# A layer with 32 experts on one core: expert lists from a table, biases with 128 rows, weight splits of 2048 columns, steps in pairs of PSUM banks

## The chip, the core and the metric

One core of a Trainium2 chip runs the whole layer in one launch. The metric is the device time in microseconds (us). The engines are TensorE (PE: matmuls, with their weight loads shown apart as PEld), VectorE (DVE), ScalarE (ACT), GpSimd (POOL) and SyncE (SP, which issues most of the transfers). Each runs its own instructions in order.

## What is computed

A sequence of 1024 tokens of width 1024 goes through a mixer (a state-space scan beside windowed attention) and then through a mixture of experts. The change concerns the experts only:

```
logits = xf @ w_router + b_router                     # 1024 tokens, 32 experts
top_v, top_i = top_k(logits, 4);  gates = softmax(top_v)
# for each expert e, over the tokens that chose it (sorted by expert, in blocks of 128)
gu = xb @ w_gate_up[e] + b_gate_up[e]                 # 1024 x 2048
glu, lin = split(gu);  glu = min(glu, 7);  lin = clip(lin, -7, 7)
act = glu * sigmoid(1.702 * glu) * (lin + 1)
y = act @ w_down[e] + b_down[e]                       # 1024 x 1024
out[token] += y * gate
```

All in float32; the kernel keeps that precision on PE by splitting each operand into a high and a low part and taking three products of them.

## The kernel before

The mixer, the router and the ranking of the experts by their counts of tokens take the first 1100 us or so. Then `moe` goes through the 32 experts in the order `ORDER`, which takes by turns one with many tokens and one with few. CAPS gives each rank its number of rows: 15 experts have more than 128 (two row blocks, "wide"), 17 have 128 ("narrow"). The last three of the order are narrow.

Each expert is 12 steps, c = 0 to 11: eight for gate and up, four for down. A step works on one chunk of weights of 1 MB. `Weights.fetch` brings a chunk in two halves (buffers raw, eight of them, filled by SP's transfers), and `Weights.prepare` in step c makes the parts of chunk c + 3: for each half of 1024 columns ACT copies hi (L1491) and DVE subtracts to get lo (L1493). The parts have four buffers, so the hi of a step begins when PE is through with the product of the step before.

In a narrow expert the rows are the stationary operand: `up` (L1306, L1307, L1309 in `product`) multiplies the chunk into one bank of PSUM, two steps to a bank, 12 matmuls of 512 columns a step. A bias matmul ends the second of them (L1320, 64 rows: hi and lo parts of 32 biases, picked by the column `pick`). `act` then reads the bank: after a gate bank ACT takes the sigmoid (L1339) and DVE multiplies (L1341); after an up bank DVE clips and multiplies (L1344, L1345), which gives um. In steps 5 and 9 PE transposes um (`turn`, L1277), and ACT and DVE split it into `a` (L1284, L1286). `down` multiplies `a` with the down weights, and `store` scales y by the gate and g2 (L1440) and adds the rows to acc_d by a scatter of POOL (L1442). In steps 1, 6, 7 and 10 PE transposes the next expert's rows x, which POOL has gathered (L1255). In a wide expert the weights are stationary (`up_wide`, L1359 and L1360, two banks a step), and `act_wide` reads the two banks in the step after.

The list of an expert (which tokens, where to add, gates) is made two experts ahead: `places` compares positions with iota on DVE (L1197, eight operations), `slots` multiplies this with the table info on PE (L1213, 8 matmuls of 6 columns for a narrow expert, 16 for a wide one) and sums up with seven small DVE operations for each row block (L1217 to L1226).

The order of PE, DVE and ACT within the stage is the order in which the code is written (a manual schedule): in each step `before`, then a `weave` of the store, `after`, `prepare` and the split of x, then `main`. `weave` takes one piece of each job by turns. The waits between engines are set by tile: an instruction that writes a tile waits for those that still read what it holds. PSUM holds eight banks: five for the products (pool emm), two for transposes (etp), one for slots (elg).

## Time and profile before

| | |
|---|---|
| median of 3 runs | 2746.44 us (2744.35 to 2754.49) |
| the profiled execution | 2748.94 us, span 2746.8 us |
| PE busy in the span | 2513.2 us (91%), 14030 matmuls |
| DVE busy | 2190.4 us (80%) |
| ACT busy | 1471.6 us (54%) |
| POOL busy | 273.7 us (10%) |
| transfers | 662.57 MB, mean 241 GB/s |

Shares over the whole span mix stages with different limits, so they say little. The expert stage lies between about 1105 and 2680 us, and is to be read by itself, in windows of it and in the timeline of one expert. A matmul's duration in a row is longer than the distance to the next one, since they are pipelined: what a matmul costs is read from start to start.

### The profile page before, as it was taken

The page shows a single profiled execution, that of the slowest core. Times are in us where ns is not written, and L with a number is a line of the kernel's source. Part 1 is how long each engine was busy: PE and PEld are TensorE (multiplying, and loading weights), DVE is VectorE, ACT ScalarE, POOL GpSimd, SP SyncE. Part 2 cuts the span into 40 slices and gives each one's busy share as a digit, 9 for nine tenths or more (in the row PEclk, how much of TensorE's full clock was granted, in tenths as well). Part 3 has the DMA queues.
Part 4 walks back from the last instruction along what each step waited for, and adds up shares of the span by engine and source line. Part 5 has one row for each costly group of instructions (what it writes and reads, how often), then busy time and mean ns, then how long its engine had stood idle before and what let it go on. Part 6 is the DMA issues. An engine that isn't in the chain of part 4 may idle for free. (4 is left out here: it accounts for less than half of the span.)

```text
span 2746.8 us, 41465 instructions
## 1 busy us (share of the span) xinstructions
PE 2513.2 (91%) x14030; PEld 2113.3 (77%) x14030; DVE 2190.4 (80%) x4354; ACT 1471.6 (54%) x2394; POOL 273.7 (10%) x173
## 2 busy tenths in 40 slices
PE   6799999889989886899999999999999999999990
PEld 1598887767778775788878878888988887888770
DVE  9735797348787757787987987988989899989995
ACT  0622112657766312555665665666666666666661
POOL 3300000000000004010100100111011011101113
PEclk8799999999999876899999999999999999999995
DMA  7434623644686782797987987998998999899984
GB/s 250 163 121 145 209 92 114 181 160 156 229 303 242 278 294 97 238 287 218 299 266 239 306 271 243 308 300 252 301 305 269 288 310 306 274 298 303 311 279 146
DMA packets 400937, 662.57 MB, mean 241 GB/s; under 512 B 36976, under 2 KB 203760, under 8 KB 393616
## 3 DMA queue, kind: packets, MB, share of 16 engines
q1 hardware_dynamic: 388416, 615.83, 67.0%
q0 software_dynamic: 11872, 42.47, 6.7%
q8 instruction: 112, 1.84, 0.3%
q10 hardware_dynamic: 432, 1.57, 0.2%
q14 instruction: 105, 0.86, 0.1%
HBM read 570.63 MB, written 89.15 MB: 240 GB/s over the span
## 5 line engine op out<-in xcount | busy, mean ns | idle before, releaser
L1493 DVE TENSOR_TENSOR wl<-raw,wh 128x1024 fp32r<-128x1024 f32 x768 | 921.6, 1220 | 162.4 <-ACT wh L1491 161.4
L1491 ACT ACTIVATE wh<-raw 128x1024 fp32r<-128x1024 f32 x768 | 789.6, 1052 | 244.0 <-PE dn L1309 88.7
L1359 PE MATMUL uw<-x,wh 128*128 128x320 f32 (+5 forms) x1920 | 578.3, 365 | 0.2 <-issue 0.2
L1360 PE MATMUL uw<-x,wl 128*128 128x192 f32 (+4 forms) x1920 | 500.2, 261 | 0.0
L1359 PEld LDWEIGHTS uw<-x,wh 128*128 128x128 f32 x1920 | 363.1, 189 | 23.5 <-issue 0.3
L1360 PEld LDWEIGHTS uw<-x,wl 128*128 128x128 f32 x1920 | 368.2, 192 | 0.5
L1306 PE MATMUL dn<-wh,a 128*128 128x512 f32 (+4 forms) x752 | 298.7, 397 | 0.0
L1307 PE MATMUL dn<-wl,a 128*128 128x512 f32 (+4 forms) x752 | 293.5, 390 | 0.0
L1309 PE MATMUL dn<-wh,a 128*128 128x512 f32 (+3 forms) x608 | 238.5, 392 | 0.6 <-DVE a L1286 0.6
L1306 PE MATMUL up<-wh,x 128*128 128x512 f32 x544 | 221.8, 408 | 0.0
L1442 POOL DMA_INDIRECT acc_d<-y,wi x47 | 118.9, 2531 | 959.5 <-DVE y L1440 815.8
L1309 PE MATMUL up<-wh,x 128*128 128x512 f32 x544 | 213.0, 392 | 0.0
L1307 PE MATMUL up<-wl,x 128*128 128x512 f32 x544 | 212.3, 390 | 0.0
L1371 ACT ACTIVATE t<-uw,bias 128x160 f32<-128x160 f32 (+5 forms) x240 | 98.6, 419 | 131.8 <-PE uw L1360 130.9
L1306 PEld LDWEIGHTS dn<-wh,a 128*128 128x128 f32 (+4 forms) x752 | 135.7, 180 | 37.8 <-issue 4.1
L1307 PEld LDWEIGHTS dn<-wl,a 128*128 128x128 f32 (+4 forms) x752 | 135.8, 181 | 33.8
L1309 PEld LDWEIGHTS dn<-wh,a 128*128 128x128 f32 (+3 forms) x608 | 112.8, 186 | 28.4 <-DVE a L1286 2.7
L1306 PEld LDWEIGHTS up<-wh,x 128*128 128x128 f32 x544 | 102.3, 188 | 27.4 <-issue 8.4
L1309 PEld LDWEIGHTS up<-wh,x 128*128 128x128 f32 x544 | 102.1, 188 | 22.4
L1307 PEld LDWEIGHTS up<-wl,x 128*128 128x128 f32 x544 | 102.4, 188 | 18.8
L51 PE MATMUL mm<-whi,uh 128*128 128x256 f32 x320 | 108.4, 339 | 4.4 <-DVE r L307 4.4
L52 PE MATMUL mm<-wlo,uh 128*128 128x256 f32 x320 | 107.7, 337 | 0.0
(529 smaller groups left out, 4970.7 us busy)
## 6 DMA issues: line engine op xcount, KB each, us to landing
raw<-w_gate_up SPq DMA_DIRECT2D x512, 512.0 KB
raw<-w_down SPq DMA_DIRECT2D x256, 512.0 KB
mw<-w_mod SPq DMA_DIRECT2D x64, 256.0 KB
raw<-w_in SPq DMA_DIRECT2D x13, 1024.0 KB
whi<-wo SPq DMA_DIRECT2D x10, 1024.0 KB
wlo<-wo SPq DMA_DIRECT2D x10, 1024.0 KB
raw<-w_mod SPq DMA_DIRECT2D x8, 1024.0 KB
gate_d<-gs SPq DMA_DIRECT2D x16, 512.0 KB
```

The source lines that it names most:

```text
L51: nc.tensor.matmul(out, lhsT=lsel(lh, k), rhs=rsel(rh, k), start=start and k == 0, stop=False)
L52: nc.tensor.matmul(out, lhsT=lsel(lh, k), rhs=rsel(rl, k), start=False, stop=False)
L1306: nc.tensor.matmul(ps, lhsT=h, rhs=wh[:, k], start=st, stop=False)
L1307: nc.tensor.matmul(ps, lhsT=h, rhs=wl[:, k], start=False, stop=en and nb <= 64)
L1309: nc.tensor.matmul(ps, lhsT=X[:, k0 + k, lo:lo + nb], rhs=wh[:, k], start=False, stop=en)
L1359: nc.tensor.matmul(p[:, 0:2 * n], lhsT=wh[:, k, fs], rhs=self.x[:, k, 0:2 * n], start=k == 0, stop=False)
L1360: nc.tensor.matmul(p[:, 0:m], lhsT=wl[:, k, fs], rhs=self.x[:, k, 0:m], start=False, stop=k == KT - 1)
L1371: nc.scalar.activation(out=y[i], in_=self.uw[i][:, 1], func=ACTF.Identity, bias=self.bias[:, q * 8 + j0 + i:q * 8 + j0 + i + 1])
L1442: nc.gpsimd.indirect_dma_start(out=K.acc_d, out_offset=bass.IndirectOffsetOnAxis(ap=wi[0:nb], axis=0), in_=o[0:nb], in_offset=None, bounds ...
L1491: nc.scalar.activation(out=h, in_=r, func=ACTF.Copy)
L1493: nc.vector.tensor_tensor(l, r, h, ALU.subtract)
```

## The change

- **Lists.** A table list_d in DRAM with 1280 rows of four numbers for each expert is filled with a default at the start. `spread`, in pieces between the steps of the first experts, computes on DVE where each token stands in the lists of its four experts, and POOL scatters the rows (32 scatters of 128 rows of 16 bytes; each waits for the one before). From the seventh expert on, the list is read from the table by one transfer of SP for each row block, and `places` and `slots` are not called. The first six are made as before.
- **Biases.** The bias operands get 128 rows in place of 64, the upper 64 zero.
- **lo.** The two halves of hi stay, the two subtractions become one of 2048 columns after both. The raw buffers hold whole chunks: four in place of eight halves.
- **Pairs.** The products' PSUM becomes three tiles of two banks. `up` writes its first bank in steps 0, 1 (4, 5) and its second in steps 2, 3 (6, 7); a narrow `down` writes the two halves of y to the two banks of one tile; `up_wide` fills one tile a step, and `act_wide` handles both banks by one operation where it had two. The extra bank for slots is gone.

```diff
+    K.list_d = dram.tile([32 * LIST, 4], I32, name="list_d")
...
+LIST = 1280
+FIRST = 6
...
+    nc.sync.dma_start(out=K.list_d, in_=a["lists"])
...
+def spread(tc, K, pool):
...
+    v.scalar_tensor_tensor(key, K.posr, 0.0, base.unsqueeze(1).to_broadcast([128, 8, 32]), ALU.is_gt, ALU.mult)
...
+    for t in range(8):
+        yield
+        v.tensor_tensor(oh, key[:, t].unsqueeze(1).to_broadcast([128, 4, 32]), mx[:, t, 0:4].unsqueeze(2).to_broadcast([128, 4, 32]), ALU.is_equal)
+        v.tensor_tensor(oh, oh, K.gr[:, t].unsqueeze(1).to_broadcast([128, 4, 32]), ALU.mult)
+        yield
+        v.reduce_sum(pay[:, t, :, 2].bitcast(F32), oh, axis=AX.X)
+        for j in range(4):
+            nc.gpsimd.indirect_dma_start(out=K.list_d, out_offset=bass.IndirectOffsetOnAxis(ap=idx[:, t, j:j + 1], axis=0),
+                                         in_=pay[:, t, j], in_offset=None, bounds_check=32 * LIST - 1, oob_is_err=True)
+            yield
...
-            s = P.pk.tile([64, 256], F32R, tag="pk", name="pk")
-            nc.vector.tensor_scalar(s, K.full, self.pick, None, ALU.mult)
-            self.sel = s[:, 0:128] if self.n == 128 else s[:, 128:256]
+            self.sel = P.pk.tile([128, 128], F32R, tag="pk", name="pk")
+            nc.vector.tensor_scalar(self.sel, K.full, self.pick, None, ALU.mult)
...
+    def banks(self, name):
+        return self.K.mm.tile([128, 2, 512], F32, tag="mm", name=name)
...
-        if c % 2 == 0:
-            self.gu = K.mm.tile([128, 512], F32, tag="mm", name="up")
-        p = self.gu
+        if c % 4 == 0:
+            self.both = self.banks("up")
+        p = self.gu = self.both[:, c // 2 % 2]
...
-        for i in range(2):
-            v.tensor_tensor(x[i], self.uw[i][:, 0], y[i], ALU.add)
+        v.tensor_tensor(x, uw[:, :, 0:n], y, ALU.add)
...
-            self.y.append([self.K.mm.tile([128, 512], F32, tag="mm", name="dn")[0:nb if nb > 64 else 2 * nb] for nb in self.blocks])
+            if self.wide or c == 0:
+                self.dn = self.banks("dn")
+            self.y.append([self.dn[0:nb if nb > 64 else 2 * nb, b if self.wide else c] for b, nb in enumerate(self.blocks)])
...
-        for i in range(2):
-            ks = slice(i * kn, (i + 1) * kn)
-            h, l, r = (x.rearrange("p k n -> p (k n)") for x in (hi[:, ks], lo[:, ks], self.raw.pop(0)))
-            nc.scalar.activation(out=h, in_=r, func=ACTF.Copy)
-            h = h.bitcast(F32)
-            nc.vector.tensor_tensor(l, r, h, ALU.subtract)
-            yield
+        h, l, r = (x.rearrange("p k n -> p (k n)") for x in (hi, lo, raw))
+        for i in (0, 1024):
+            nc.scalar.activation(out=h[:, i:i + 1024], in_=r[:, i:i + 1024], func=ACTF.Copy)
+            if i == 0:
+                yield
+        nc.vector.tensor_tensor(l, r, h.bitcast(F32), ALU.subtract)
+        yield
...
-    P.ahead = 8 if deep else 4
+    P.ahead = 4 if deep else 2
...
-        K.mm = pool(es, "emm", 5, space=PSUM)
+        K.mm = pool(es, "emm", 3, space=PSUM)
         K.tp = pool(es, "etp", 2, space=PSUM)
-        K.lg = pool(es, "elg", 1, space=PSUM)
...
+                    nc.sync.dma_start(out=x[0:nb], in_=K.list_d[r * LIST + b * 128:r * LIST + b * 128 + nb])
...
-                        weave(prev.store(1) if c == 0 and prev else None, cur.after(c), W.prepare(), x)
+                        weave(prev.store(1) if c == 0 and prev else None, cur.after(c), W.prepare(), x, limit(to_lists, 2))
```

The order of instructions shows what the pairs do. A name has its buffer's number behind it, and what stands in brackets is the engines or queues that the instruction waits for. **PE, from step 5 to step 6 of a narrow expert, before:**

```order
L1307 MATMUL up_23162<-wl_23098,x_22386 128x512
L1309 MATMUL up_23162<-wh_23097,x_22386 128x512
L1320 MATMUL up_23162<-bgu_10327,pk_22966 128x512
L1277 MATMUL tp_23226<-ident_60,x_22894 128x128 [waits PE_49]
L1277 MATMUL tp_23226<-ident_60,x_22894 128x128 x3
L1306 MATMUL up_23246<-wh_23130,x_22386 128x512 [waits Activation_49]
```

**And in the change**, the same place (L1361 is the bias matmul, L1315 the transposes of the next x, L1344 the first matmul of `main`):

```order
L1345 MATMUL up_21361<-wl_21312,x_20726 128x512
L1347 MATMUL up_21361<-wh_21311,x_20726 128x512
L1361 MATMUL up_21361<-bgu_10330,pk_21187 128x512
L1315 MATMUL tp_21404<-ident_60,x_21121 128x128 [waits PE_49]
L1315 MATMUL tp_21404<-ident_60,x_21121 128x128 x3
L1344 MATMUL up_21361<-wh_21332,x_20726 128x512 [waits DVE_49]
```

The product of step 6 had a tile of its own (up_23246) and its first matmul waited for ACT's hi; now it goes to the other bank of the tile up_21361 that the bias has just finished, and it waits for DVE. From step 1 to step 2 it is the same without the transposes.

**PE, from step 10 to step 11 of the same expert, before:**

```order
L1306 MATMUL dn_23306<-wh_23268,a_23065 128x512
L1307 MATMUL dn_23306<-wl_23269,a_23065 128x512
L1309 MATMUL dn_23306<-wh_23268,a_23065 128x512
L1306 MATMUL dn_23336<-wh_23296,a_23065 128x512
L1307 MATMUL dn_23336<-wl_23297,a_23065 128x512
```

**And in the change:**

```order
L1344 MATMUL dn_21477<-wh_21442,a_21282 128x512
L1345 MATMUL dn_21477<-wl_21443,a_21282 128x512
L1347 MATMUL dn_21477<-wh_21442,a_21282 128x512
L1344 MATMUL dn_21477<-wh_21468,a_21282 128x512 [waits DVE_49]
L1345 MATMUL dn_21477<-wl_21469,a_21282 128x512
```

The second half of y had a tile of its own (dn_23336) and no wait at its first matmul; now both halves are in dn_21477, and the first matmul of step 11 waits for DVE.

**DVE, from step 1 to step 2 of the same expert, before:**

```order
L1493 TENSOR_TENSOR wl_22006<-raw_21891,wh_22005 128x1024 [waits DMAHW2_49,Activation_49]
L1493 TENSOR_TENSOR wl_22006<-raw_21893,wh_22005 128x1024 [waits DMAHW3_49,Activation_49]
L1286 TENSOR_TENSOR x_21994<-tp_21995,x_21994 128x4x128 [waits PE_49]
L1493 TENSOR_TENSOR wl_22033<-raw_21925,wh_22032 128x1024 [waits DMAHW4_49,PE_49,Activation_49]
L1341 TENSOR_TENSOR t_22026<-up_21981,t_22026 128x512
L1493 TENSOR_TENSOR wl_22033<-raw_21927,wh_22032 128x1024 [waits DMAHW5_49,Activation_49]
```

**And in the change** (L1531 is lo, L1324 the lo part of the next x, L1382 the multiplication by the sigmoid):

```order
L1531 TENSOR_TENSOR wl_21287<-raw_21179,wh_21286 128x2048 [waits DMAHW4_49,DMAHW5_49,PE_49,Activation_49]
L1324 TENSOR_TENSOR x_21276<-tp_21277,x_21276 128x4x128 [waits PE_49]
L1382 TENSOR_TENSOR t_21306<-up_21263,t_21306 128x512 [waits Activation_49]
L1531 TENSOR_TENSOR wl_21312<-raw_21211,wh_21311 128x2048 [waits DMAHW6_49,DMAHW7_49,PE_49,Activation_49]
L1531 TENSOR_TENSOR wl_21333<-raw_21244,wh_21332 128x2048 [waits DMAHW0_49,DMAHW1_49,PE_49,Activation_49]
```

Ahead of L1382 stood half a lo of its own step, and half of the one before; now a whole lo of the step before and the copy of x stand there, and the lo of its own step comes behind it.

## Rows read from the trace of the kernel before

**Rows 1.** Windows: one stretch of the expert stage, with the columns.
```profile
core 0: us, PE busy (x) PEld busy (x) DVE busy (x) ACT busy (x) POOL busy (x), PEclk, DMA share, GB/s
1200.00:1400.00 200.00, 199.12 (x1049) 165.51 (x1048) 166.47 (x290) 118.32 (x168) 17.93 (x11) 1.00 0.84 265
```

**Rows 2.** PE's waits, 1150 to 2680 us: in total, times, longest.
```profile
PE tp L1277 <- DVE t L1345: 4.6, 15, 0.3
```

**Rows 3.** Windows over one narrow expert, 2002.38 to 2041.83, the sum.
```profile
sum 39.45, PE 39.15 PEld 30.20 DVE 38.47 ACT 28.16 POOL 6.09; mean PE 9.79 PEld 7.55 DVE 9.62 ACT 7.04 POOL 1.52
```

**Rows 4.** Timeline of PE around a bias matmul (start, duration in us).
```profile
2008.08 0.39 PE L1309 MATMUL up<-wh,x 128*128 128x512 f32 x1
2008.39 0.49 PE L1320 MATMUL up<-bgu,pk 64*128 64x512 f32 x1
...
2009.15 0.39 PE L1307 MATMUL up<-wl,x 128*128 128x512 f32 x1
...
2011.89 0.39 PE L1307 MATMUL up<-wl,x 128*128 128x512 f32 x1
```

**Rows 5.** Windows, PE at the slots matmuls (L1213) alone, from the seventh expert's list.
```profile
1340.00:2600.00 1260.00, 23.99 (x304) 1.00 0.90 284
```

**Rows 6.** Timeline of PE: transposes of um behind a slots group, next matmul.
```profile
2018.41 0.66 PE L1277 MATMUL tp<-ident,t 128*128 128x128 f32 x4 [0.30 <-DVE t L1345]
2018.83 0.47 PE L1306 MATMUL up<-wh,x 128*128 128x512 f32 x1
```

**Rows 7.** Timeline of DVE in the same narrow expert.
```profile
2007.64 2.35 DVE L1493 TENSOR_TENSOR wl<-raw,wh 128x1024 fp32r<-128x1024 f32 x2
2009.91 0.68 DVE L1286 TENSOR_TENSOR x<-tp,x 128x512 fp32r<-128x512 f32 x1
2010.51 1.21 DVE L1493 TENSOR_TENSOR wl<-raw,wh 128x1024 fp32r<-128x1024 f32 x1
2011.64 0.68 DVE L1341 TENSOR_TENSOR t<-up,t 128x512 f32<-128x512 f32 x1
...
2041.55 0.74 DVE L1440 SCALAR_TENSOR_TENSOR y<-dn,gt,g 128x512 f32<-128x512 f32 x1
```

**Rows 8.** Timeline of ACT in the same narrow expert.
```profile
2005.36 1.06 ACT L1491 ACTIVATE wh<-raw 128x1024 fp32r<-128x1024 f32 x1 [0.48 <-ACT wh L1491]
...
2006.94 1.05 ACT L1491 ACTIVATE wh<-raw 128x1024 fp32r<-128x1024 f32 x1
2008.92 0.60 ACT L1339 ACTIVATE t<-up 128x512 f32<-128x512 f32 x1 [0.93 <-PE up L1320]
...
2019.11 0.60 ACT L1284 ACTIVATE a<-tp 128x512 fp32r<-128x512 f32 x1 [2.51 <-PE tp L1277]
2019.60 2.00 ACT L1491 ACTIVATE wh<-raw 128x1024 fp32r<-128x1024 f32 x2
```

**Rows 9.** Timeline of PE: two idle times of the mixer (in brackets).
```profile
288.70 0.35 PE L51 MATMUL mm<-whi,uh 128*128 128x256 f32 x1 [2.53 <-DVE r L307]
...
501.46 0.68 PE L458 MATMUL yp<-wo,ss 128*128 128x128 f32 x4 [1.92 <-DMA wo<-wout_d]
```

**Rows 10.** Windows with the granted clock (PEclk): behind these two, and in the expert stage.
```profile
288.70:292.10 3.40, 3.40 (x18) 3.40 (x19) 2.56 (x7) 0.00 (x0) 0.00 (x0) 0.58 0.57 147
501.50:505.00 3.50, 3.50 (x27) 3.32 (x28) 0.75 (x2) 0.76 (x1) 0.00 (x0) 1.00 0.69 214
1873.00:1876.50 3.50, 3.50 (x15) 3.50 (x14) 3.15 (x10) 1.88 (x4) 1.07 (x1) 0.51 0.86 267
```

**Rows 11.** Timeline of POOL: lists of the third expert done; the third expert's scatter.
```profile
1147.61 1.00 POOL L1255 DMA_INDIRECT x<-xm_d,ri  x1 [31.46 <-DVE L L1217]
...
1296.03 2.33 POOL L1442 DMA_INDIRECT acc_d<-y,wi  x1 [34.87 <-DVE y L1440]
```

**Rows 12.** POOL's gathers (L1255), then its adding scatters (L1442): issue to landing.
```profile
DMA to landing us min/median/max: 4.0/5.9/8.2
...
DMA to landing us min/median/max: 6.0/9.5/12.7
```

More of the change, by code (lines that the diff above doesn't have):

```diff
@@ L1101, in rank_consts @@
     K.eid = late.tile([1, 32], I32, name="eid")
-    K.pick = late.tile([64, 32], F32, name="pick")
+    K.pick = late.tile([128, 32], F32, name="pick")
+    v.memset(K.pick[64:128], 0.0)
     K.cnt = late.tile([64, 32], F32, name="cnt")
@@ L1186, in rank_gates @@
     v.tensor_copy(gr, p)
+    K.gr = pool.tile([128, 8, 32], F32, bufs=1, name="gr0")
+    nc.scalar.activation(out=K.gr, in_=p, func=ACTF.Copy)
     for j in range(3):
@@ L1335, in act @@
         nc, P, nb = self.nc, self.P, self.n
-        x = self.whole(self.gu, nb, ("hg", "hu")[q])[0:nb]
-        t = P.tmp.tile([128, 512], F32, tag=("sg", "um")[q], name="t")[0:nb]
+        x = self.gu[0:nb]
+        t = P.tmp.tile([128, 2, 512], F32, tag=("sg", "um")[q], name="t")[0:nb, 0]
         if q == 0:
@@ L1353, in up_wide @@
         wh, wl = w
-        self.uw = []
+        t = self.banks("uw")
         for i in range(2):
-            p = K.mm.tile([128, 512], F32, tag="mm", name="uw")
+            p = t[:, i]
             fs = slice(i * 128, (i + 1) * 128)
@@ L1461, in add @@
         for m, kn, k, c in WIDE if wide else CHUNKS:
-            self.todo += [(eid, m, kn // 2, k + i * kn // 2, c) for i in range(2)]
+            self.todo.append((eid, m, kn, k, c))
     def fetch(self):
@@ L1473, in fetch @@
         w = w.rearrange("e (p k) n -> p (e k) n", p=128) if m == "w_gate_up" else w.rearrange("e (k p) n -> p (e k) n", p=128)
-        nc.sync.dma_start(out=r, in_=w[:, k:k + kn])
+        for h in range(0, kn, kn // 2):
+            nc.sync.dma_start(out=r[:, h:h + kn // 2], in_=w[:, k + h:k + h + kn // 2])
         self.raw.append(r)
@@ L1586, in expert_consts @@
     nc = tc.nc
-    K.bgu = late.tile([64, 2 * D], F32R, name="bgu")
-    K.full = late.tile([64, 256], F32, name="full")
+    K.bgu = late.tile([128, 2 * D], F32R, name="bgu")
+    K.full = late.tile([128, 128], F32, name="full")
     nc.gpsimd.memset(K.full, 1.0)
-    nc.gpsimd.memset(K.full[:, 192:256], 0.0)
-    br = K.wp.tile([128, KT, 256], F32, tag="raw", name="br").rearrange("p k n -> p (k n)")[0:64]
+    br = K.wp.tile([128, KT, 256], F32, tag="raw", name="br").rearrange("p k n -> p (k n)")
+    nc.gpsimd.memset(br[64:128], 0.0)
     for j in range(2):
         nc.sync.dma_start(out=br[j * 32:(j + 1) * 32], in_=a["b_gate_up"])
-    nc.gpsimd.tensor_scalar(br[:, D:], br[:, D:], 1.0, 1.0, ALU.add, ALU.mult)
+    nc.gpsimd.tensor_scalar(br[0:64, D:], br[0:64, D:], 1.0, 1.0, ALU.add, ALU.mult)
     for c in range(4):
@@ L1618, in expert_id, with table @@
                 if r not in regs:
-                    regs[r] = nc.sync.value_load((eid if P.ahead == 8 else K.eid)[0:1, r:r + 1], min_val=0, max_val=31)
+                    regs[r] = nc.sync.value_load((eid if P.ahead == 4 else K.eid)[0:1, r:r + 1], min_val=0, max_val=31)
                 return regs[r]
             def place(i):
-                if i < len(ORDER):
+                if i < FIRST:
                     r = ORDER[i]
                     return places(tc, K, P.li, lambda t: K.posr[:, t, r:r + 1], CAPS[r])
+            def table(r):
+                out = []
+                for b, nb in enumerate(BLOCKS[CAPS[r]]):
+                    x = P.li.tile([128, 4], I32, tag="tab%d" % b, name="tab")
+                    nc.sync.dma_start(out=x[0:nb], in_=K.list_d[r * LIST + b * 128:r * LIST + b * 128 + nb])
+                    out.append((x[:, 0:1], x[:, 1:2], x[:, 2:3].bitcast(F32)))
+                yield out
             def lists(i, o, *steps):
@@ L1629, in lists @@
                     r = ORDER[i]
-                    return slots(tc, K, P.li, K.lg, o, lambda t: K.info[:, t, r, :], BLOCKS[CAPS[r]], *steps)
+                    return table(r) if i >= FIRST else slots(tc, K, P.li, K.tp, o, lambda t: K.info[:, t, r, :], BLOCKS[CAPS[r]], *steps)
             def start(i, ls):
@@ L1638, in start @@
                 return e
-            P.ahead = 2
+            P.ahead = 1
             with tc.manual_schedule(engines={mybir.EngineType.PE, mybir.EngineType.DVE, mybir.EngineType.Activation}):
@@ L1648, in moe @@
                 regs.clear()
-                P.ahead = 8
+                P.ahead = 4
                 for x in cur.x_parts():
@@ L1658, in moe @@
             prev = None
+            to_lists = spread(tc, K, P.li)
             with tc.manual_schedule(engines={mybir.EngineType.PE, mybir.EngineType.DVE, mybir.EngineType.Activation}):
@@ L1748, in rest @@
             v.tensor_copy(inf[:, :, 3:6], K.info[:, :, 0, 3:6])
-            pk = sm.tile([64, 1], F32, tag="pk", name="pk")
-            v.tensor_tensor(pk, K.route[0:64, 65:66], row[0:64, 33:34], ALU.is_equal)
+            pk = sm.tile([128, 1], F32, tag="pk", name="pk")
+            v.memset(pk[64:128], 0.0)
+            v.tensor_tensor(pk[0:64], K.route[0:64, 65:66], row[0:64, 33:34], ALU.is_equal)
             W = Weights(tc, a, P)
             W.add(eid)
-            e = Expert(tc, K, P, (128,), pk, next(slots(tc, K, P.li, K.lg, places(tc, K, P.li, lambda t: pos[:, t:t + 1], 128),
+            e = Expert(tc, K, P, (128,), pk, next(slots(tc, K, P.li, K.tp, places(tc, K, P.li, lambda t: pos[:, t:t + 1], 128),
                                                         lambda t: inf[:, t, :], (128,))))
```

64 lines of the change are left out of this document (38 added, 26 removed).

## The prediction

> **What bounds the kernel now.** I read the windows of the expert stage first. TensorE (PE) is busy 199.12 of 200 us at the full clock, VectorE (DVE) 166.47, ScalarE (ACT) 118.32 [rows 1]. The list of PE's waits over the whole stage has one entry worth naming, 4.6 us in 15 places, none over 0.3 us [rows 2]. So the stage is PE's queue laid end to end: time is won only by taking something off that queue, and whatever makes PE wait is added in full. In a narrow expert (39.45 us) DVE is busy 38.47 us as well [rows 3]. The reader should keep that in mind: a new wait of PE on DVE meets an engine with a full queue.
>
> **The change, part by part.** The sum is made against the profiled execution, 2748.94 us, which is 2.5 us above the median of the three runs.
>
> *Bias with 128 rows.* A plain matmul of 512 columns costs 0.228 us: twelve of them start between 2009.15 and 2011.89. From the last one before a 64-row bias matmul (2008.08) to the second one after it (2009.15) are 1.07 us, where three plain ones take 0.68 [rows 4]. So 0.39 us is lost around it. There are 4 in each of 17 narrow experts; with 128 rows I take it that they become plain matmuls: 68 x 0.39 = **-26.2 us**.
>
> *Lists from the table.* From the seventh expert on, the slots matmuls go: 304 in the rows, 23.99 us of PE [rows 5], **-24.0**. With them goes most of the wait in front of the transposes of um, 0.30 us where it is shown [rows 6]; of the 4.6 us I take **-4.0**. places and the small list operations leave DVE, which gives no time by itself, as PE does not wait for them. What spread adds to DVE lies in the first three experts, where DVE has 33 us free in 200 [rows 1]: nothing, and if that cover were gone, at most its own length on DVE. The fill of list_d is one early transfer. SP's 38 table reads stand among the weight fetches of step 5 and wait for the last scatter alone, which must have landed long before the fifth expert: nothing on SP, nothing for the fetches behind them. The 32 scatters of GpSimd (POOL) are a rival, below.
>
> *lo in one piece of 2048 columns.* Two pieces of 1024 take 2.27 us from start to start (2007.64 to 2009.91), one of 512 takes 0.60 (2009.91 to 2010.51) [rows 7]: 0.065 fixed plus 0.535 for each 512, so 2.21 for 2048. The 0.06 saved is DVE's, not PE's: nothing. But the piece starts only after both halves of hi. At the very first chunk nothing hides that: one half of hi, 1.06 [rows 8], **+1.1**. A raw buffer now comes free by whole chunks, one half piece (1.1 us) later; with four chunks ahead, some 13 us of a narrow expert's steps [rows 3], that is nothing.
>
> *Steps in pairs of PSUM banks.* Here the order tells more than the diff. up now puts two products in one tile of two banks, and down puts both halves of y in one. The waits are set for a tile as a whole. So the matmul that opens bank 1 waits for whoever reads bank 0, although it writes nowhere near. In a narrow expert that happens three times: main(2) opens bank 1 while DVE's L1382 (t<-up,t of step 2) must still read bank 0; the same at main(6); and main(11) opens bank 1 of dn while L1476 (y<-dn of step 11) must still read bank 0. Before, main(6) and main(11) had no wait for DVE there at all, and main(2) only an old one. PE is in order, so everything behind the waiting matmul stands: the rest of main, and through the weight buffers the hi of a later step. A wide expert reads its pairs a step later and gets no such wait; its merged operations only spare DVE and ACT instructions, which PE does not wait for: nothing.
>
> What is late: L1382 stands on DVE behind the lo of the step before and behind a copy of x, and that lo stands behind two halves of hi on ACT, which begin when the product before the last one ends. I lay this out from the start s of that product's last matmul, with 0.04 us for a hand-over (bias 2008.39 + 0.49 to the sigmoid at 2008.92).
> - Step 2: matmul 0.39 + 0.04, hi, copy of x and hi 2.63 (2005.36 to 2006.94 + 1.05), 0.04, lo 2.21, copy 0.60, L1382 0.68, 0.04: 6.63 [rows 4, 7, 8]. PE is there at 0.23 + transposes 0.42 + main 2.74 + bias 0.23 = 3.62 [rows 4, 6]. It stands **3.0**.
> - Step 6: the copy of a starts 0.70 after the transposes of um, and two hi end 3.19 after them, so 3.42 after s; 0.04 + lo 2.21 + L1382 0.68 + 0.04 gives 6.39, against 0.23 + 0.42 + 2.74 + 0.23 + 0.42 = 4.04 [rows 4, 6, 7, 8]: **2.35**.
> - Step 11: as step 2, with L1476's 0.74 for L1382: 6.69, some 0.5 less for the smaller copies there, against 0.23 + 0.42 + 2.74 = 3.39 [rows 4, 6, 7, 8]: **2.75**, an estimate.
>
> Together 8.1 us for each narrow expert, 17 x 8.1 = **+137.7**. Bounds: were DVE free each time, only bias, sigmoid and L1382 would follow each other (0.49 + 0.04 + 0.60 + 0.04 + 0.68 + 0.04 - 0.23, 1.6; 1.2 at step 6; 1.0 at step 11), 3.8 in all, +65. Were DVE as late as it is today (L1341 ends 3.93 us after the bias starts, so 3.93 + 0.04 - 0.23 = 3.74; the same at step 11, 0.42 less at step 6), it would be 10.8, +184 [rows 4, 7]. I take the worked-out value: DVE's 38.47 us of work then lie in some 47 [rows 3], so it is no longer late by its queue, and only the chain through hi holds.
>
> *The clock.* PE does not idle in this stage today. After an idle time of 2.53 us the next 3.4 us ran at a granted clock of 0.58; after one of 1.92 us the next 3.5 us ran at 1.00 [rows 9, 10]. Of the two levels, 1.2 and 2.4 GHz, the lower costs half of 3.4, 1.7 us. My three stops leave PE idle about 2.9, 2.2 and 2.6 us; I count one drop and a half for each narrow expert, 25 x 1.7 = **+43** (bounds: none, 0, and all 51, +87). The one drop of the stage today (0.51 for 3.5 us at 1873, after a slots group) goes with the slots: **-1.7** [rows 10].
>
> Sum: -26.2 - 24.0 - 4.0 + 1.1 + 137.7 + 43 - 1.7 = +126, 2875 against the profiled time, **2872 us** against the median.
>
> **The rivals.**
> - *The pair does not hold PE* (faster). As data, the two banks of a pair have nothing to do with each other. If main(2), main(6) and main(11) can start before the reads of bank 0 end, only the gains stay: -26.2 - 24.0 - 4.0 - 1.7 + 1.1 = -54.8, **2692 us**. The place is the first matmul of these products; it decides as soon as L1382 ends less than 0.23 us after the bias matmul starts, that is before PE comes by. For it: the wide experts lose nothing, and a per-bank wait is all that the data need. Against: the order has the wait on DVE where there was none, and even with DVE free the sigmoid and L1382 alone take 1.9 us from the bias. The Trainium skill, page "PSUM — Partial Sum Buffer", section "PSUM bank collisions raise a hardware error", says that readers and matmuls need guarding by bank (and quadrant), and that another bank may be read while a matmul runs; no run here shows it, and by it alone the wait is one the program imposes, not the chip. I give 0.06.
> - *DVE is in time* (shortest stops): +65 - 54.8, and with stops of 1.0 to 1.6 us no clock is lost: **2756 us**. It needs lo to be off DVE before the bias ends, against the chain through hi above. 0.05.
> - *The stops come, the clock holds*: **2829 us**, for it the 1.92 us that cost nothing [rows 9, 10]. 0.15; it is part of the forecast's range.
> - *POOL's scatters are late.* Each of the 32 waits until the one before has landed, and the gathers for the fifth expert stand behind all of them. From their start in the first expert (the gather at 1147.61 marks its step 5) to the fourth expert's start (the scatter of y at 1296.03, plus 8 us of stops) there are some 153 us, less 8 for the gathers' own landing: 4.5 us a scatter is the limit. Landings of gathers take 4.0 to 8.2, of adding scatters 6.0 to 12.7 [rows 11, 12]. The table's rows are of 16 bytes against 4 KB, so they are nearest to the 4.0, within the limit. At 5.9 it would cost 32 x 1.4 = 45: **2917 us**; 0.08.
> - *The bias does not do what it should*: 128 rows cost what 64 do. Then 26.2 are not won: **2898 us**; 0.08. For the forecast speaks that the 0.39 us lie on both sides of the matmul [rows 4], as if PE changed over. The Trainium skill, page "TensorE: Matmul & The Clock Gate", section "Why this matters for your kernels", gives a single matmul of few rows the time of one of 128; by that the lost time would stay. The rows differ: 0.49 against 0.39 us for this matmul alone.
>
> **How the numbers follow.** Forecast 0.58 (clock partly lost), with the held clock, the late POOL and the idle bias on the same side (0.31), the shortest stops 0.05, faster 0.06. The range takes in the held clock less a third of the stops and, above, all drops and POOL's middle price: 2785 to 2940. About 0.5%, 13.7 us, is what a measurement of this kernel can tell from no change. Faster 0.06, same 0.05, slower 0.89.
>
> **What would show it.** PE's list of waits, empty today, must show up<-DVE t (L1382) some 34 times and dn<-DVE y (L1476) 17 times, 2 to 3 us each, 100 to 150 us together. A narrow expert must take about 45 us, or 47 to 48 with the drops, instead of 39.45; a wide one no longer than today less its slots group. PE's busy share in the windows falls most late in the stage. The row around a bias must be 0.23 apart on both sides. If the waits are missing, or under 1 us, the forecast is wrong and the time falls below today's; if PE waits for x<-xm_d at the fourth expert, it was POOL.

## The result, and the profile after

| | before | after |
|---|---|---|
| median | 2748.0 us (4 runs) | 2975.33 us (4 runs, 2970.46 to 2981.73) |
| ratio | | 1.083 (95% interval 1.081 to 1.084) |
| span of the profiled execution | 2746.8 us | 2979.9 us |
| PE busy | 2513.2 us | 2566.9 us |
| DVE busy | 2190.4 us | 2089.3 us |

The change makes the kernel 8.3% slower. It was forecast slower, at 2872 us, 2785 to 2940; the time lies beyond the upper end. DVE has 100 us less to do, as the change says, and the time does not follow it.

The list of PE's waits in the changed kernel, from 1090 us on (total, times, longest), to be set beside [rows 2]:

```profile
PE up L1344 <- DVE t L1382: 97.4, 34, 6.0
PE dn L1344 <- DVE y L1476: 39.4, 17, 3.0
PE tp L1315 <- DMA x<-xm_d,ri: 22.7, 2, 13.4
PE dn L1347 <- DVE a L1428: 16.3, 9, 2.3
PE tp L1315 <- DVE x L1324: 12.6, 3, 9.7
PE up L1344 <- ACT wh L1528: 8.9, 1, 8.9
PE tp L1315 <- DVE t L1386: 3.4, 9, 0.8
PE up L1345 <- DVE wl L1531: 2.8, 1, 2.8
```

The first two lines are the forecast stops: 34 at L1382 and 17 at L1476, 136.8 us of idle time (a "stop" is from here on such a wait of PE). The other lines were not in the forecast: 16.3 us in wide experts (L1428 makes the low part of `a`), and at the start 22.7 us for the rows x (9.3 of them for the second expert's rows; the kernel before waited 8.2 for its rows), 12.6 us for the low part of x (7.6 before), 8.9 and 2.8 us for weights. All waits of PE from 1090 us on, with 2.0 us under "issue", make 205.5 us; in the kernel before they make 21.2.

One stop, the one at step 2 of a narrow expert, row by row in the timelines of three engines (start, duration, in brackets the idle time in front and what ended it). PE:

```profile
1469.33 0.40 PE L1347 MATMUL up<-wh,x 128*128 128x512 f32 x1
...
1472.53 0.40 PE L1347 MATMUL up<-wh,x 128*128 128x512 f32 x1
1472.76 0.40 PE L1361 MATMUL up<-bgu,pk 128*128 128x512 f32 x1
1475.83 0.50 PE L1344 MATMUL up<-wh,x 128*128 128x512 f32 x1 [2.67 <-DVE t L1382]
```

ACT in the same time, the two halves of hi (the copy of x lies between them) and the sigmoid:

```profile
1469.76 1.06 ACT L1528 ACTIVATE wh<-raw 128x1024 fp32r<-128x1024 f32 x1 [0.72 <-PE up L1347]
...
1471.21 1.05 ACT L1528 ACTIVATE wh<-raw 128x1024 fp32r<-128x1024 f32 x1
1473.20 0.60 ACT L1380 ACTIVATE t<-up 128x512 f32<-128x512 f32 x1 [0.94 <-PE up L1361]
```

DVE, with lo, the copy and L1382:

```profile
1472.29 2.29 DVE L1531 TENSOR_TENSOR wl<-raw,wh 128x2048 fp32r<-128x2048 f32 x1 [0.26 <-ACT wh L1528]
1474.50 0.69 DVE L1324 TENSOR_TENSOR x<-tp,x 128x512 fp32r<-128x512 f32 x1
1475.10 0.68 DVE L1382 TENSOR_TENSOR t<-up,t 128x512 f32<-128x512 f32 x1
```

The product of step 0 issues its last matmul at 1469.33. 0.43 us later hi begins, and it ends 2.93 us after that matmul's start. lo, the copy and L1382 follow each other without a gap, and PE starts 0.05 after L1382 ends. The sigmoid (1473.20) has been done for 1.3 us by then: the chain runs through hi and lo, as worked out, and ends after 6.50 us (6.63 forecast). The bias matmul is now 0.23 behind its neighbour, against 0.31 in [rows 4]. Behind the stop, from 1477.07 on, the matmuls start 0.43 apart in place of 0.23: the clock.

Not every stop at step 2 is like this one. From 1926 us on it takes 3.3 to 4.9 us in nine narrow experts. They are those that follow a wide expert whose second block has 64 rows or fewer, and the store of such a block has an operation more on ACT and one on DVE (hg, a part of that block's y). The stop at 1926.97, in the timelines of ACT, DVE and PE:

```profile
1919.00 0.59 ACT L1369 ACTIVATE hg<-dn 64x512 f32<-64x512 f32 x1 [2.19 <-DVE y L1476]
...
1923.45 2.27 DVE L1531 TENSOR_TENSOR wl<-raw,wh 128x2048 fp32r<-128x2048 f32 x1
...
1926.25 0.67 DVE L1382 TENSOR_TENSOR t<-up,t 128x512 f32<-128x512 f32 x1
...
1926.97 0.65 PE L1344 MATMUL up<-wh,x 128*128 128x512 f32 x1 [4.92 <-DVE t L1382]
```

From the lo that starts at 1920.57 to the end of L1382 DVE has no idle time. So here DVE is late by its queue, and not by the chain through hi alone. The nine stops take 12.3 us more than 2.67 us each would.

The windows of the changed kernel (the stretch and its length; busy time of PE, PEld, DVE, ACT and POOL; then the granted clock PEclk, DMA share, GB/s), for the start of the expert stage, for the rest of it, and for the 3.6 us behind the stop at 1475.83:

```profile
1105.00:1440.00 335.00, 277.61 (x1379) 231.42 (x1380) 216.42 (x308) 156.68 (x206) 72.92 (x47) 0.89 0.66 203
1440.00:2860.00 1420.00, 1292.28 (x6664) 1095.99 (x6663) 1029.61 (x956) 799.27 (x1073) 127.56 (x75) 0.95 0.80 256
1476.40:1480.00 3.60, 3.60 (x10) 2.83 (x9) 1.61 (x1) 0.00 (x0) 0.30 (x1) 0.53 0.97 270
```

The kernel before, in the same two parts of its stage:

```profile
1105.00:1440.00 335.00, 326.27 (x1697) 269.73 (x1694) 276.40 (x492) 199.97 (x277) 31.14 (x18) 0.98 0.82 260
1440.00:2640.00 1200.00, 1195.73 (x6665) 1018.44 (x6664) 1072.81 (x1976) 781.24 (x1125) 132.86 (x72) 1.00 0.91 289
```

The third number from the right is the mean granted clock. 0.05 of 1420 us is 71 us lost to the lower of the two levels, 1.2 GHz, where nothing was lost before; in the first 335 us it is 0.11, 37 us, where 0.02, 7 us, were lost before. Of the 45 stops that begin after 1440 us all but the last take 2.0 us or more. Behind 35 of these 44 the clock of the next 3.5 us is 0.69 or less; behind the other nine it is 1.00. Two stops on PE's timeline that come out against their length:

```profile
2291.17 0.50 PE L1344 MATMUL dn<-wh,a 128*128 128x512 f32 x1 [2.00 <-DVE y L1476]
```

```profile
2468.13 0.50 PE L1344 MATMUL up<-wh,x 128*128 128x512 f32 x1 [3.34 <-DVE t L1382]
```

And the windows of the 3.5 us behind each:

```profile
2291.17:2294.67 3.50, 3.50 (x11) 2.80 (x12) 2.29 (x1) 0.04 (x1) 0.00 (x0) 0.68 1.04 363
2468.13:2471.63 3.50, 3.50 (x15) 2.90 (x16) 2.14 (x1) 0.37 (x1) 0.77 (x1) 1.00 0.84 249
```

After 2.00 us of idle time the clock is at 0.68, after 3.34 us at 1.00: the length of the one stop does not decide alone.

A narrow expert, 1466.84 to 1517.53, takes 50.7 us where it took 39.45 [rows 3] and 47 to 48 were forecast; DVE is busy 36.57 of them, by the sum of its windows:

```profile
sum 50.69, PE 42.50 PEld 33.43 DVE 36.57 ACT 27.84 POOL 7.53; mean PE 21.25 PEld 16.72 DVE 18.29 ACT 13.92 POOL 3.76
```

The start is the other loss. By the scatter of the fourth expert (1400.38 us against 1335.68) the changed kernel is 65 us behind. Six of the forecast stops, 20.2 us, and the slow clock behind them are part of that. The timeline of POOL there, with the gather of the fourth expert's rows (1258.77, between scatters), the last scatters into the table and the gather of the fifth expert's rows:

```profile
1258.77 1.06 POOL L1294 DMA_INDIRECT x<-xm_d,ri  x1 [0.30 <-issue]
...
1308.62 0.99 POOL L1264 DMA_INDIRECT list_d<-lp,li  x1 [5.02 <-DMA list_d<-lp,li]
...
1325.14 0.98 POOL L1264 DMA_INDIRECT list_d<-lp,li  x1 [1.97 <-DMA list_d<-lp,li]
1326.42 1.06 POOL L1294 DMA_INDIRECT x<-xm_d,ri  x1 [0.30 <-issue]
```

In the kernel before the fourth expert's rows were gathered at 1205.97. PE stands for them here:

```profile
1263.47 1.09 PE L1315 MATMUL tp<-ident,x 128*128 128x128 f32 x4 [13.37 <-DMA x<-xm_d,ri]
```

SP's queue in its timeline, where nothing went out between 1292.92 and the first of these lines:

```profile
1327.80 3.70 SPq L1668 DMA_DIRECT2D tab<-list_d  x8
1332.34 3.59 SPq L1511 DMA_DIRECT2D raw<-w_gate_up  x6
```

The 32 scatters start between 1169.79 and 1325.14, one in 5.0 us; the forecast put the limit at 4.5, for the gathers of the fifth expert; PE's wait came at those of the fourth, which stand in the middle of the scatters. And SP holds eight table reads in one go (1327.80), which wait for the last scatter; the weight fetches behind them go out at 1332.34, and PE waits 8.9 us (to 1337.37) and 2.8 us (to 1340.94) for weights.

### The profile page after: what moved, and what is told of

Read it like the earlier page. It is cut to its first block, busy times and chain, and to the rows that moved or that the text cites. A ratio compares the mean times of both kernels' runs of the same rounds, so it can differ in the third digit from the quotient of the medians.

```text
span 2979.9 us, 39138 instructions
## 1 busy us (share of the span) xinstructions
PE 2566.9 (86%) x13726; PEld 2157.1 (72%) x13726; DVE 2089.3 (70%) x3146; ACT 1450.4 (49%) x2275; POOL 308.9 (10%) x205
## 5 line engine op out<-in xcount | busy, mean ns | idle before, releaser
L1531 DVE TENSOR_TENSOR wl<-raw,wh 128x2048 fp32r<-128x2048 f32 x384 | 878.5, 2290 | 442.2 <-ACT wh L1528 440.8
L1344 PE MATMUL dn<-wh,a 128*128 128x512 f32 (+4 forms) x752 | 311.3, 414 | 39.4 <-DVE y L1476 39.4
L1344 PE MATMUL up<-wh,x 128*128 128x512 f32 x544 | 241.5, 444 | 106.3 <-DVE t L1382 97.4
L1345 PE MATMUL dn<-wl,a 128*128 128x512 f32 (+4 forms) x752 | 305.7, 407 | 0.0
L1347 PE MATMUL dn<-wh,a 128*128 128x512 f32 (+3 forms) x608 | 250.2, 411 | 16.3 <-DVE a L1428 16.3
L1345 PE MATMUL up<-wl,x 128*128 128x512 f32 x544 | 232.0, 426 | 2.8 <-DVE wl L1531 2.8
L1347 PE MATMUL up<-wh,x 128*128 128x512 f32 x544 | 232.4, 427 | 0.0
L1344 PEld LDWEIGHTS up<-wh,x 128*128 128x128 f32 x544 | 114.3, 210 | 141.5 <-DVE t L1382 108.4
L1344 PEld LDWEIGHTS dn<-wh,a 128*128 128x128 f32 (+4 forms) x752 | 142.2, 189 | 83.3 <-DVE y L1476 46.5
L1294 POOL DMA_INDIRECT x<-xm_d,tab x38 | 67.9, 1786 | 690.2 <-PE tp L1315 650.1
L1345 PEld LDWEIGHTS up<-wl,x 128*128 128x128 f32 x544 | 114.5, 211 | 26.5 <-DVE wl L1531 3.3
L1347 PEld LDWEIGHTS up<-wh,x 128*128 128x128 f32 x544 | 113.9, 209 | 26.9
L1478 POOL DMA_INDIRECT acc_d<-y,tab x38 | 61.5, 1617 | 660.7 <-DVE y L1476 509.1
```

The source lines that it names most:

```text
L1294: nc.gpsimd.indirect_dma_start(out=x[0:nb], out_offset=None, in_=K.xm_d, bounds_check=S - 1, oob_is_err=True, in_offset=bass.IndirectOffse ...
L1344: nc.tensor.matmul(ps, lhsT=h, rhs=wh[:, k], start=st, stop=False)
L1345: nc.tensor.matmul(ps, lhsT=h, rhs=wl[:, k], start=False, stop=en and nb <= 64)
L1347: nc.tensor.matmul(ps, lhsT=X[:, k0 + k, lo:lo + nb], rhs=wh[:, k], start=False, stop=en)
L1478: nc.gpsimd.indirect_dma_start(out=K.acc_d, out_offset=bass.IndirectOffsetOnAxis(ap=wi[0:nb], axis=0), in_=o[0:nb], in_offset=None, bounds ...
L1531: nc.vector.tensor_tensor(l, r, h.bitcast(F32), ALU.subtract)
```

## The experiments

Four questions: is it the shared tile that stops PE; what is the clock worth; what is behind the loss at the start; and where are the gains, since 55 us of them were counted?

**Single tiles in narrow experts.** The pairs stay in wide experts.

```diff
-        if c % 4 == 0:
-            self.both = self.banks("up")
-        p = self.gu = self.both[:, c // 2 % 2]
+        if c % 2 == 0:
+            self.gu = self.banks("up")[:, 0]
+        p = self.gu
...
-            if self.wide or c == 0:
-                self.dn = self.banks("dn")
-            self.y.append([self.dn[0:nb if nb > 64 else 2 * nb, b if self.wide else c] for b, nb in enumerate(self.blocks)])
+            self.dn = self.banks("dn")
+            self.y.append([self.dn[0:nb if nb > 64 else 2 * nb, b] for b, nb in enumerate(self.blocks)])
```

> The changed kernel, but in narrow experts each product gets a tile of its own again (the first bank of a pair); wide experts keep their pairs. Theory (the wait is set because two products share a tile): the 34 stops at L1382 and the 17 at L1476, 136.8 us in the changed kernel, go, and with them the clock drops behind them, some 47 of 3.4 us at half clock, about 80 us; 2755 us, between 2740 and 2785; the stops at the start (rows x, first weights after the table reads) and those of wide experts at L1428 stay. Rival (three buffers in place of five make PE wait for DVE wherever the tile is, since DVE is late by its queue): the stops move to other products of narrow experts, not below 2930.

Measured: 2820.34 us, 155 less than the changed kernel, ratio to before 1.026 (1.024 to 1.029). PE's list of waits in this run:

```profile
PE tp L1315 <- DVE t L1386: 39.8, 30, 4.2
PE tp L1315 <- DMA x<-xm_d,ri: 29.0, 2, 19.8
```

Not one wait at L1382 or L1476 is left, so the shared tile made them: there are three buffers here as in the changed kernel, and only the sharing of a tile by two products is gone. But 39.8 us of waits for um (L1386), 3.4 in the changed kernel, have come up in their place: with the large stops gone PE reaches the next thing that DVE is late with. The time is 65 us above the forecast for this run; 36 of them are these waits, and the rest was not taken apart.

**Fillers for PE in the stops.** Nine plain matmuls of constants ahead of each of the 51 waiting matmuls; their result goes nowhere.

```diff
+        if not self.wide and c in (2, 6, 11):
+            p = self.K.tp.tile([128, 512], F32, tag="tp", name="fill")
+            for _ in range(9):
+                self.nc.tensor.matmul(p, lhsT=self.sel, rhs=self.K.bgu[:, 0:512], start=True, stop=True)
```

> The changed kernel (2975 us) with nine plain matmuls of constants, 2.05 us, put on PE ahead of each of the 51 matmuls that wait; their result is used nowhere. They lie inside the stops of 2.0 to 4.9 us. Theory (after each stop PE runs 3.4 us at half the clock, which costs 1.7 us): no stop leaves PE idle for more than 1 us except the longest, some 40 drops go, 70 us: 2905 us, faster with 459 more matmuls. Rival (the drops cost nothing, as DVE sets the pace in these experts anyway): 2970 or more.

Measured: 2920.98 us, 54 us faster than the changed kernel with 459 matmuls more. Its window of the expert stage, which is shorter here:

```profile
1440.00:2800.00 1360.00, 1315.34 (x6976) 1116.45 (x6975) 1021.45 (x948) 792.17 (x1063) 130.75 (x75) 0.99 0.83 266
```

And PE's list of waits:

```profile
PE up L1344 <- DVE t L1382: 25.3, 18, 3.0
...
PE dn L1344 <- DVE y L1480: 4.9, 7, 0.9
```

The granted clock of the stage is 0.99, and 30.2 us of the 136.8 are left as idle time. The stops are about as long as before, they are only filled: 51 times 2.05 us and 30.2 make 134.8. The time lies between the two theories, nearer to the first, and the second falls. So some 55 to 70 us of the changed kernel are the clock's: 54 gained here, and 71 less the 14 that 0.99 still costs make 57 by the windows.

**lo in two pieces, pairs kept.**

```diff
+            nc.vector.tensor_tensor(l[:, i:i + 1024], r[:, i:i + 1024], h[:, i:i + 1024].bitcast(F32), ALU.subtract)
+            yield
-            if i == 0:
-                yield
-        nc.vector.tensor_tensor(l, r, h.bitcast(F32), ALU.subtract)
-        yield
```

> The changed kernel with lo in two pieces of 1024 columns again, each right behind its half of hi; pairs and table stay. Theory (each stop is the chain hi, lo, copy, L1382 from the end of an earlier product): half a lo, 1.1 us, leaves each of the 51 stops, 56 us; the 16.3 us at L1428 of wide experts go too, and some of the clock drops: 2840 to 2900 us, stops of 1.0 to 1.9 us. Rival (DVE is late because its queue is full, so the split does not matter): 2965 or more, stops as before.

Measured: 2991.47 us, 16 more than the changed kernel; the 51 stops take 192.5 us in PE's list of waits:

```profile
PE up L1344 <- DVE t L1382: 141.6, 34, 9.3
PE dn L1344 <- DVE y L1476: 50.9, 17, 3.5
```

The time is in the rival's range, but its stops "as before" are not there: both theories had it wrong, the first because it left the order out. The timeline of DVE at one stop, of step 6:

```profile
1469.05 2.47 DVE L1529 TENSOR_TENSOR wl<-raw,wh 128x1024 fp32r<-128x1024 f32 x2
1471.43 0.68 DVE L1382 TENSOR_TENSOR t<-up,t 128x512 f32<-128x512 f32 x1
```

And that of PE, the matmul behind the stop (the bias matmul ahead of it starts at 1468.28):

```profile
1472.27 0.76 PE L1344 MATMUL up<-wh,x 128*128 128x512 f32 x1 [3.14 <-DVE t L1382]
```

With two pieces `weave` puts the first piece of the step's own lo ahead of L1382 (two pieces stand there from 1469.05, L1382 behind them), and that piece can only begin when the product just done has freed its buffer. The chain got a later starting point, not a shorter one. One whole lo behind L1382 was the better order for these stops. The wait at L1428 went from 16.3 to 0.9 with the same edit (there a low part of `a` had stood behind the whole lo). PE's wait for x went from 22.7 to 7.6, with the same scatters at the same pace; why the fourth expert's rows come in time here was not looked into.

**Table reads from ACT in place of SP**, on top of single tiles.

```diff
-                    nc.sync.dma_start(out=x[0:nb], in_=K.list_d[
+                    nc.scalar.dma_start(out=x[0:nb], in_=K.list_d[
```

> The run with single tiles (2820 us), with the table reads issued from ACT at their own step in place of SP. Theory (eight table reads stand ahead of weight fetches on SP and wait there for the last scatter): PE's waits for the first weights after them, 10.0 and 2.8 us, and the clock drop of 17 us with them (8.5 us) go: 2799 us. Rival (the weights are late for another reason): the wait stays, 2815 or more.

Measured: 2804.04 us, 16 less. PE's waits for weights are gone from its list. ACT's order is that of the code, so a read stands there at its step; SP's is made by a scheduler, which had put eight of them together and early. The wait for x rose from 29.0 us, by PE's list of waits:

```profile
PE tp L1315 <- DMA x<-xm_d,ri: 49.1, 3, 22.3
```

One wait of 17.5 us, to 1344.43, is new: with the weights on time PE comes to the fifth expert's rows, whose gathers stand on POOL behind the last scatter. All listed waits make 110 us, against 111 in the run with single tiles, so the list does not show where the 16 us were won.

**Half the pace for the scatters**, on top of that. One piece of `spread` a step, table from the ninth expert on.

```diff
-FIRST = 6
+FIRST = 8
...
-weave(prev.store(1) if c == 0 and prev else None, cur.after(c), W.prepare(), x, limit(to_lists, 2))
+weave(prev.store(1) if c == 0 and prev else None, cur.after(c), W.prepare(), x, limit(to_lists, 1))
```

> The run before this one, with one piece of spread a step in place of two and the lists of two more experts made in the old way. Theory (the gather of x stands on POOL behind scatters that each wait for the one before): the wait of 19.8 us for x and its clock drop (10 us) go, the two lists cost 2.5: 2772 us. Set against the run with all three undone (2728 us), which differs by lo in two pieces alone, it gives the price of lo in one piece: some 45 us, from stops at L1386 and L1428. Rival (lo in one piece is free, the rest of the 92 us between those two runs lay at the start): 2735 or less.

Measured: 2761.21 us, 43 less than the run before it. The wait for x falls from 49.1 to 9.8 us, nearly all of it for the second expert's rows, which was there before the change. The scatters themselves are no quicker: they land after 5.9 us in the median, and one starts every 6.4. But four of them stand on POOL ahead of the gather of the fourth expert's rows (1223.73), where there are 15 in the changed kernel. The two steps together are worth 59 us in the kernel with single tiles: the start. What is left in PE's list of waits:

```profile
PE tp L1315 <- DVE t L1386: 29.6, 31, 2.3
PE dn L1347 <- DVE a L1428: 16.8, 9, 2.3
```

**All three undone:** single tiles, reads from ACT at half the pace, and now lo in two pieces, on top of the run before.

```diff
-            if i == 0:
-                yield
-        nc.vector.tensor_tensor(l, r, h.bitcast(F32), ALU.subtract)
-        yield
+            nc.vector.tensor_tensor(l[:, i:i + 1024], r[:, i:i + 1024], h[:, i:i + 1024].bitcast(F32), ALU.subtract)
+            yield
```

> The changed kernel with single tiles in narrow experts, lo in two pieces, the table reads issued from ACT at their own step in place of SP, the scatters at half the pace and the lists of two more experts made in the old way. By the theories of the three causes (pairs, one piece of lo, table reads and scatters that hold up SP and POOL) all stops of the changed kernel are gone and only its gains are left: 2690 to 2710 us. Rival (merged operations or the three pairs cost something by themselves): 2740 or more.

Measured: 2727.71 us, ratio 0.992 (0.989 to 0.994): faster than before, though neither theory's number. Against the run before it lo in one piece costs 33 us once PE no longer stands at the pairs. In the lists of waits 16 of them are the waits for the low part of `a` (16.8 to 0.6) and 2 those for um (29.6 to 27.2, now 17 times, 2.0 at most); the rest was not taken apart.

**um a step later**, on top of that.

```diff
-TURN = 5, 9
+TURN = 6, 9
```

> The run with all three undone (2728 us), with um transposed first in step 6 in place of step 5. Theory (um is late by one place in DVE's queue): most of the 27 us at L1386 go, 2705 us, the fastest so far. Rival (DVE is full in narrow experts, so that what PE saves comes back at the next point where it needs DVE): the wait moves to the second um or to the down products, 2722 or more.

Measured: 2740.7 us, 13 more. The time is the rival's: the wait for um went from 27.2 to 4.8, and another came, in PE's list of waits:

```profile
PE tp L1315 <- DVE a L1324: 23.8, 14, 2.7
```

It is not where the rival put it. Step 6 now transposes um and rows x, which fills both transpose tiles, and the transposes of step 7 wait until DVE has read the low part of `a` out of one of them. That DVE is full and that the tiles are too few are both possible; this run does not tell them apart.

**Raw weights in halves**, on top of all three undone: the class Weights of the kernel before, with eight raw buffers.

```diff
-        n = 2048 // kn
+        n = 1024 // kn
...
-    P.ahead = 4 if deep else 2
+    P.ahead = 8 if deep else 4
```

> The run with all three undone (2728 us), with the raw weights in eight buffers of half a chunk again, as before the change. Theory (its 27 us of PE's waits for um come from DVE's queue running late, and that partly from ACT, which waits 31 us for whole raw chunks between 1450 and 2650): ACT's waits for raw go, PE's waits for um fall below 15, 2714 us. Rival (DVE's queue is full by its own work): no change, 2724 or more.

Measured: 2727.2 us, no change. ACT's waits for raw weights fell, as expected, from 30.8 to 10.6 us between 1450 and 2650, but PE's for um stayed (26.7). The theory falls. The list of waits of all engines in this run shows a better one:

```profile
ACT hg L1369 <- DVE y L1475: 43.2, 18, 2.8
```

For hg ACT copies a part of a wide expert's second block out of bank 1 of the pair (where the block has 64 rows or fewer), and DVE scales the first block out of bank 0. Both only read, and still ACT waits for DVE: 43.2 us here and in the run before, 17.9 us in the changed kernel. In the kernel before, and in the run with table and bias below, where each bank is a tile of its own, this wait is not there at all. So it is the shared tile again, here between two readers. That DVE is late for um because of it is the likely reason and not shown: no run took this wait away alone.

**The bias alone**, in the kernel before: 128 rows for pick, bgu, full and the selection.

```diff
-    K.bgu = late.tile([64, 2 * D], F32R, name="bgu")
+    K.bgu = late.tile([128, 2 * D], F32R, name="bgu")
```

> The kernel before with the 128-row biases alone. Theory (0.39 us is lost around each of 68 bias matmuls of 64 rows): 26 us faster, 2720 us, ratio 0.990, and about 0.23 us from start to start around the bias. Rival (a matmul of 64 rows takes what one of 128 takes): no difference, ratio between 0.998 and 1.002.

Measured: 2743.18 us, ratio 0.998 (0.997 to 0.999), a quarter of what was counted. The matmul itself did what was expected: the next one starts 0.23 after it, and from the matmul ahead of it (2007.82) to the second one behind it (2008.52) are 0.70 us, where it was 1.07 [rows 4]. The rival, whose ratio this is, falls with that. But PE's wait for um grew from 4.6 to 22.9 us. PE's timeline around one bias matmul:

```profile
2008.06 0.40 PE L1320 MATMUL up<-bgu,pk 128*128 128x512 f32 x1
2008.29 0.39 PE L1306 MATMUL up<-wh,x 128*128 128x512 f32 x1
```

PE's list of waits, to be set beside [rows 2]:

```profile
PE tp L1277 <- DVE t L1345: 22.9, 30, 1.1
```

DVE is busy 38.47 of the 39.45 us of a narrow expert [rows 3]. Of the 20 us that are missing, 18.3 stand in this wait: what PE saves comes back as a wait for DVE.

**The table alone**, in the kernel before (ninth expert on, ACT's queue, half pace).

```diff
+                    return table(r) if i >= FIRST else slots(tc, K, P.li, K.lg, o, lambda t: K.info[:, t, r, :], BLOCKS[CAPS[r]], *steps)
...
-                if i < len(ORDER):
+                if i < FIRST:
```

> The kernel before with the table alone (from the ninth expert on, read by ACT's queue, scatters at half pace). Theory (slots leave PE, and places and the list operations leave DVE in the same experts, so that the gain is not given back as that of the bias was): 20 us less on PE, no waits for um, some 6 us more at the start: 2730 us. Rival (PE waits for DVE instead, as with the bias alone): 2743 or more.

Measured: 2721.97 us, ratio 0.990 (0.988 to 0.992), 29 us, more than forecast. Places and the list operations leave DVE in the very experts where PE saves, and no wait comes back: PE's for um is 3.3 us in all.

**Table and bias**, in the kernel before, with its five single banks: the run of the table alone, and on top of it

```diff
-            self.sel = P.pk.tile([64, 128], F32R, tag="pk", name="pk")
+            self.sel = P.pk.tile([128, 128], F32R, tag="pk", name="pk")
...
-    K.bgu = late.tile([64, 2 * D], F32R, name="bgu")
+    K.bgu = late.tile([128, 2 * D], F32R, name="bgu")
```

> The run before this one with the 128-row biases added. Theory (with places and the list operations gone DVE has room in narrow experts, so that the bias's 26 us are now won): 2706 us. Rival (DVE still sets the pace): as the table alone, 2725 or more. Against the ninth run it shows what the pairs of banks in wide experts are worth by themselves.

Measured: 2703.93 us, ratio 0.984 (0.982 to 0.986), the fastest of all. The bias is now worth 18 us, as DVE has room. PE's waits for um are 8.0 us in 6 places by its list of waits, none of them after 1440 us:

```profile
PE tp L1315 <- DVE t L1383: 8.0, 6, 1.7
```

Against the run with raw halves, which has the pairs in wide experts, it is 23 us faster, and PE's waits for um are 18.7 us less: the pairs of wide experts, and the buffers that they leave, cost more than the merged operations bring. Which share lies at hg and which at the three buffers was not tried.

## Why the prediction was right or wrong

- **Where it breaks: right.** The three stops a narrow expert, at L1382 twice and at L1476, are there, 51 of them, and the two rivals without them, or with short ones, fall. Undoing the shared tile in narrow experts gave back 155 us.
- **The length of the stops: right in sum, in part by luck.** Like with like, 136.8 us of idle time stand against 2.9, 2.2 and 2.6 in each of 17 experts, 130.9; the 137.7 are the time from start to start, which is some 0.17 a stop longer. Step 2 takes 3.6 in the mean, step 6 2.2, step 11 2.3. In six experts step 2 takes 2.67, as in the stop shown, where only the chain through hi acts. That DVE "is no longer late by its queue" fails in the nine experts behind hg (3.3 to 4.9 us); their excess, 12.3 us, is offset in part by stops that are shorter elsewhere.
- **The clock: mis-sized, the largest miss.** "I count one drop and a half for each narrow expert", 43 us. From 1440 us on the windows give 71 us, and the fillers gained 54 with part of the idle time left; with the start it is 108, against 7 before. The step counted drops by the length of a stop, and of the stops of 2.0 to 2.1 us 16 in 20 had one behind them. The waits at the start, which were put at nothing, brought drops too.
- **The table on SP and POOL: wrong.** "Nothing on SP, nothing for the fetches behind them" failed: the order has eight reads together ahead of weight fetches, which were taken to lie among them at step 5. And the late scatters, a rival at 0.08, came true, with its sign (PE waits for x at the fourth expert): "nearest to the 4.0" was wrong, landings took 4.7 us in the median, and one scatter started every 5.0. In the changed kernel PE waits 13.4 us for x and 11.7 us for weights because of the two; undone, they are worth 59 us in the kernel with single tiles.
- **lo in one piece: wrong.** "+1.1" counted the first chunk only. In wide experts the low part of `a`, which PE waits for, stands on DVE behind the whole lo: 16.3 us in the changed kernel, 33 us of time where nothing else hides it.
- **"A wide expert ... gets no such wait": wrong.** PE gets none from the pairs there, but ACT does at hg, 17.9 us in the changed kernel and 43.2 where PE no longer stops.
- **The bias, -26.2: not there by itself** (-6), since DVE is full in narrow experts; with the lists gone, 18. The profile had said so, and the text quoted it [rows 3] and did not use it.
- **The lists, -24 and -4: right**, 29 us alone, and that with two more lists made in the old way.
- **The range** was said to take in "all drops and POOL's middle price"; the two together (44 and 45 on top of 2872) make 2961 us, not 2940. The time lies above that too.

The median is 103 us above the forecast, the profiled execution 107 above its 2875. The profiles give a count: PE's waits grew by 184 us where the forecast has 135 (137.7, 1.1 and -4.0), 50 too few; the clock took 101 us more where it has 41 (43 and -1.7), 60 too few. Together that is 110. The count is rough, since the lower clock can also fall into a wait.

What stays open: why a stop is mostly followed by the lower clock and sometimes not, be it 2.07 or 3.34 us long; and how the waits at a tile are set, since at hg a reader waits for a reader, and since ACT waits for the two halves of a raw buffer one by one (in the run with all three undone, 1.26 and 0.52 us at 1545.13 and 1546.70), while the two banks of a pair are not told apart.

## What to carry to other kernels

Merging buffers into one tile merges their waits, writer against reader and reader against reader; before two banks share a tile, look for a place where one is written or read while the other is, and look in the order for a new wait there. Time saved on PE in a stretch where another engine is as busy is not won until that engine is relieved in the same stretch. And a transfer that waits for a late result is better placed on a queue whose order is written by hand than ahead of weight fetches on one that a scheduler orders.

## What the runs showed of the hardware

459 matmuls more made the kernel 54 us faster, as they kept PE at the higher level of the clock through its stops (0.99 against 0.95). A bias matmul with 64 rows costs 0.37 to 0.39 us more around it than one with 128, though it does less: 1.07 us from the matmul ahead of it to the second one behind it [rows 4], against 0.70 with 128 rows. And scatters of 128 rows of 16 bytes land after 2.1 to 8.0 us, median 4.7: not much sooner than gathers of 4 KB rows (4.0 to 8.2, median 5.9), though in half the time of the scatters that add 4 KB rows (median 9.5) [rows 12]. The view of line L1264 of the changed kernel alone:

```profile
DMA to landing us min/median/max: 2.1/4.7/8.0
```
